# Dense products that read their moving operand in turn from its two halves

## The chip, the cores and the metric

The kernel runs on one core of one Trainium2 chip. The metric is the time of one execution in device microseconds (us); shorter is better. TensorE does the matrix products, VectorE, ScalarE and GpSimd the rest, and DMA queues bring the weights from the chip's main memory.

## The reference

A trunk of two layers works on 256 tokens of 1024 channels in float32. In each layer one input projection of the normalised stream feeds three token mixers: Mamba-2 (with a causal convolution of width 4 ahead of it), sliding-window attention with rotated queries and keys, and forgetting attention. Each has its own gate path, is projected back to 1024 channels, weighted by a sigmoid gate and summed; an output projection is added to the residual.

```python
for layer in range(DEPTH):
    h = rms_norm(x, norm_w[layer])
    proj = jnp.einsum('bsd,de->bse', h, w_in[layer])
    (a_xbc, a_z, a_dt, b_q, b_k, b_v, b_z,
     c_q, c_k, c_v, c_f, c_z, gates) = jnp.split(proj, split_at, axis=-1)
    y_a = mamba2_branch(a_xbc, a_z, a_dt, conv_w[layer], conv_b[layer], dt_bias[layer],
                        a_log[layer], d_skip[layer], ssm_norm_w[layer])
    y_b = sliding_window_branch(b_q, b_k, b_v, b_z, sinks[layer], cos, sin)
    y_c = forgetting_attention_branch(c_q, c_k, c_v, c_f, c_z, f_bias[layer])
    ys = jnp.stack([y_a, y_b, y_c], axis=2)
    branch = jnp.einsum('bsiw,iwd->bsid', ys, w_proj[layer])
    g = jax.nn.sigmoid(gates.reshape(b, s, N_BRANCH, d) + gate_bias[layer])
    merged = jnp.sum(g * branch, axis=2)
    x = x + jnp.einsum('bsd,de->bse', merged, w_out[layer])
return rms_norm(x, final_norm_w)
```

## The kernel before

Every dense product is computed to float32 accuracy from two-part operands. Weights and activations are split into a high part (type float32r) and the rest (also float32r): ScalarE copies the high part, VectorE subtracts it (`split`, lines 239 and 240). `dense` (line 254) then makes three matmuls for each of the eight blocks of 128 input channels: high by high, low by high, high by low. A product is thus 24 matmuls into one PSUM tile of the tag `mm`, of which there are three (`pmm`, line 71).

There are two orientations. `chan` (line 400) keeps 128 weight columns stationary and moves the activations, 256 tokens wide; its result has channels on the partitions and tokens along the row. The projections back (`u_proj`) do the same with the outputs of the mixers. `tok` (line 407) keeps 128 tokens stationary and moves the weights, 256 or 512 columns wide; its result has tokens on the partitions. It makes the sliding-window queries, keys and values, the values of forgetting attention, and the output projection. A small product (`u_small`) has 64 weight columns (two parts of 32) against 256 tokens. In all of them the moving operand is read word after word along a row.

Each product is followed by an eviction that reads its PSUM tile: a Tanh with a multiply-add for the gate paths (`u_z`: ScalarE line 727, then VectorE line 730 or, in the Mamba branch, 734), a Tanh for the sigmoid gates (`u_gate`, line 827), a multiply-add for the projections (`u_proj`, lines 847, 849, 855), ScalarE copies for keys, queries and values (lines 436, 773, 781, 791), the rotation (`rope`, lines 421 to 424, VectorE), and the residual sum (`u_out`, line 888, VectorE). The convolution (`u_conv`) reads the PSUM tile four times: a scaled copy with bias on ScalarE (line 640) and three multiply-adds on VectorE with the tokens shifted by 1, 2 and 3 (line 643).

TensorE's order is the program's. The dense products follow a written list (lines 938 to 1015); between them `pump` lets pieces of the attention and of the Mamba scan into TensorE's queue, by a clock that counts estimated TensorE time and by due times. The order on the other engines is the scheduler's, except at the start. Weights arrive on SP's DMA queue six pieces ahead; up to four split pieces are held. Small work tiles of 256 columns share the tag `L1`, with twelve buffers.

Of the kernel before, what the change touches and what calls it, by code (L numbers as in the profile page):

```python
# [16 lines left out]
P = 128  # L17
S = 256
# [25 lines left out]
def hybrid_trunk(  # L44
# [188 lines left out]
    def row_rstd(ss, n):  # L233
        return rsqrt(row_var(ss, n), 1)

    def split(hi, lo, src, scale=None):

        if scale is None:
            act(hi, src, AF.Copy)  # L239
            tt(lo, src, hi.bitcast(F32), op=ALU.subtract)  # L240
        else:
            act(hi, src, AF.Copy, scale=scale)  # L242
            stt(lo, src, scale, hi.bitcast(F32), op0=ALU.mult, op1=ALU.subtract)
# [156 lines left out]
    def chan(y, w, c):  # L400

        p = pmm()
        dense(p[:, 0:S], lambda k: w.hi(k)[:, c:c + P], lambda k: w.lo(k)[:, c:c + P],
              lambda k: y.hTh[:, k, :], lambda k: y.hTl[:, k, :], w)
        return p[:, 0:S]

    def tok(ah, al, w, t, p=None, **kw):

        n = w.n
        p = pmm() if p is None else p  # L410
        sl = slice(t * P, (t + 1) * P)
        dense(p[:, 0:n], lambda k: ah[:, k, sl], lambda k: al[:, k, sl], w.hi, w.lo, w,
              mid=pump if n == 512 else None, **kw)
        return p[:, 0:n]

    def rope(p, t):

# [9 lines left out]
    def u_bkv(y, c0, t, after=None):  # L427

        def f(w):
            p = tok(y.hTh, y.hTl, w, t, after=after)  # L430
            if t == 0 and c0 == 0:
                kv = T("L8", [P, 2048])
                y.kT = kv[:, 0:1024].rearrange("p (h s) -> p h s", h=4)
                y.bv = kv[:, 1024:1536].rearrange("p (t c) -> p t c", t=2)
            if c0 + w.n == 512:
                act(y.bv[:, t, :], p[:, w.n - 256:w.n], AF.Copy)
            if c0 == 0:
                a, b = rope(p[:, 0:256], t)
                kd = T("L2", [P, 4, 2, 64])
                for i in range(2):  # L440
                    gtt(kd[:, :, i, :], a, b, op=ALU.add)
                launch(1, rest(kd), D_K)
            pump()

        def rest(kd):
            pt = pmx()
            for h in range(4):
                transpose(pt[:, h * P:(h + 1) * P], kd[:, h, :, :].rearrange("p a b -> p (a b)"), ident)
            act(y.kT[:, :, t * P:(t + 1) * P], pt.rearrange("p (h s) -> p h s", h=4), AF.Copy)
            yield 0.0  # L450
        return f

    def u_bq(y, c0, t):

        def f(w):
            p = tok(y.hTh, y.hTl, w, t)
            for i in range(w.n // 256):
                if t == 0:
                    y.qT[c0 + i] = T("qt", [P, 2, S])
                a, b = rope(p[:, 256 * i:256 * i + 256], t)  # L460
                q = T("L1", [P, 4, 64])
                gtt(q, a, b, op=ALU.add)
                launch(1, rest(c0 + i, q.rearrange("p h d -> p (h d)")), D_Q)
            pump()

        def rest(c, q):
            qT = y.qT[c]
            pt = pmx()
            for j in range(2):
                transpose(pt[:, j * P:(j + 1) * P], q[:, j * P:(j + 1) * P], ident)  # L470
            act(qT[:, :, t * P:(t + 1) * P], pt[:, 0:256].rearrange("p (h s) -> p h s", h=2), AF.Copy)
            if t == 1:
                launch(1, swa_quad(y, c, qT), D_QK)
            yield 0.0
        return f
# [85 lines left out]
    def u_small(y):  # L561
        def f(w):

            p = pmm()
            for k in range(NK):
                for a in (y.hTh, y.hTl):
                    mm(p[0:64, 0:S], w.both[:, k, :], a[:, k, :], start=(k == 0 and a is y.hTh),
                       stop=(k == NK - 1 and a is y.hTl))
            raw = T("L1", [64, S])
            act(raw, p[0:64, 0:S], AF.Copy)  # L570
            launch(1, decay_logits(y, raw), 2.0)
            pump()
        return f
# [57 lines left out]
    def u_conv(y, u, c):  # L631
        def f(w):
            p = chan(y, w, c)
            if u == 8:
                y.bcT = T("L8", [P, 8, S])
            if u == 0:
                y.xs = T("L8", [P, 8, S])
            dst = y.xs[:, u, :] if u < 8 else y.bcT[:, u - 8, :]
            a = T("L1", [P, S])
            act(a, p, AF.Identity, scale=y.vec[:, 48 + u:49 + u], bias=y.vec[:, 64 + u:65 + u])  # L640
            for j in (2, 1, 0):
                s = 3 - j
                stt(a[:, s:S], p[:, 0:S - s], y.vec[:, 16 * j + u:16 * j + u + 1], a[:, s:S],  # L643
                    op0=ALU.mult, op1=ALU.add)
            th = T("L1", [P, S])
            act(th, a, AF.Tanh)  # L646
            stt(dst, th, 1.0, a, op0=ALU.add, op1=ALU.mult)
            if u < 8 and u % 2 == 1:
                launch(0, ssd_group(y, u // 2), D_G0)
            pump()  # L650
        return f
# [66 lines left out]
    def u_z(y, br, u, c):  # L718
        def f(w):
            p = chan(y, w, c)  # L720
            if u == 0 and br != 0:
                y.sz[br] = T("L8", [P, NK, S])
            if u == 0 and br == 0:
                y.yh[br] = T("L8", [P, NK, S], F32R)
                y.yl[br] = T("L8", [P, NK, S], F32R)
            th = T("L1", [P, S])
            act(th, p, AF.Tanh, scale=0.5)  # L727
            y.zdone.add(u) if br == 1 else None
            if br != 0:
                stt(y.sz[br][:, u, :], th, 1.0, p, op0=ALU.add, op1=ALU.mult)  # L730
            else:
                drain(0)
                sz = T("L1", [P, S])
                stt(sz, th, 1.0, p, op0=ALU.add, op1=ALU.mult)  # L734
                gtt(y.xs[:, u, :], y.xs[:, u, :], sz, op=ALU.mult)  # L735
                sq = T("L1", [P, S])
                act(sq, y.xs[:, u, :], AF.Square)  # L737
                y.sq.append(sq)
                if u % 2 == 1:
                    launch(3, group_norm(y, u // 2, *y.sq[-2:]), D_GN0)  # L740
            pump()
        return f
# [25 lines left out]
    def u_cv(y, c, t):  # L768
        def f(w):
            p = tok(y.hTh, y.hTl, w, t)  # L770
            if c == 0 and t == 0:
                y.cv = T("L8", [P, 2, D])
            act(y.cv[:, t, c:c + w.n], p, AF.Copy)
            pump()
        return f

    def u_ck(y, j, c):
        def f(w):
            p = chan(y, w, c)
            y.ckT[j] = T("qt", [P, 2, S])  # L780
            act(y.ckT[j][:, 0, :], p, AF.Copy)
            if j % 2 == 0:
                launch(2, fox_quad(y, j), D_FOX)
            pump()
        return f

    def u_cq(y, j, c):
        def f(w):
            p = chan(y, w, c)
            kq = y.ckT[j]  # L790
            act(kq[:, 1, :], p, AF.Copy)
            y.cqdone[j] = clock["t"]
            pump()
        return f
# [28 lines left out]
    def u_gate(y, br, u, c):  # L823
        def f(w):
            p = chan(y, w, c)
            g = T("L1", [P, S])
            act(g, p, AF.Tanh, scale=0.5, bias=y.vec[:, 88 + 8 * br + u:89 + 8 * br + u])  # L827
            y.gate[u] = g
            pump()
        return f  # L830

    def u_proj(y, br, u, c):
        def f(w):
            if u == 0:
# [3 lines left out]
                if br == 2:  # L838
# [2 lines left out]
            p = pmm()[:, 0:S]  # L841
            yh, yl = y.yh[br], y.yl[br]
            dense(p, lambda k: w.hi(k)[:, c:c + P], lambda k: w.lo(k)[:, c:c + P],
                  lambda k: yh[:, k, :], lambda k: yl[:, k, :], w)
            g = y.gate.pop(u)
            if br == 1:
                stt(y.mg[:, u, :], g, 1.0, p, op0=ALU.add, op1=ALU.mult)
            elif br == 0 or u < NK - 1:
                stt(g, g, 1.0, p, op0=ALU.add, op1=ALU.mult)  # L849
                gtt(y.mg[:, u, :], y.mg[:, u, :], g, op=ALU.add)  # L850
                if br == 2:
                    split(y.mh[:, u, :], y.ml[:, u, :], y.mg[:, u, :], scale=0.5)
            else:
                with tc.high_priority():
                    stt(g, g, 1.0, p, op0=ALU.add, op1=ALU.mult)
                    tt(y.mg[:, u, :], y.mg[:, u, :], g, op=ALU.add)
                    split(y.mh[:, u, :], y.ml[:, u, :], y.mg[:, u, :], scale=0.5)
            pump()
# [9 lines left out]
    def u_out(y, c, t, first=False, i=0):  # L868

        def f(w):  # L870
# [14 lines left out]
            else:  # L885
                p = tok(y.mh, y.ml, w, t)
            with tc.high_priority():
                tt(y.xn[:, t, sl], p, xo, op=ALU.add)
                sum_sq(y.xn, t, c, y.ss[t][:, i:i + 1], n)
                last = y.l + 1 == L  # L890
                nwb = fin["w"] if last else layers[y.l + 1].nwb
# [215 lines left out]
```

## Time and profile before

| | |
|---|---|
| median of 3 runs | 903.3 us (903.29 to 906.38) |
| profiled execution | 905.64 us, span 903.5 us |
| granted TensorE clock, mean | 0.99 |
| TensorE busy (matmul) | 884.3 us |
| VectorE busy | 628.8 us |
| ScalarE busy | 505.8 us |
| GpSimd busy | 136.0 us |
| read from main memory | 152.10 MB |

The profile gives, for one execution, the busy time of each engine, the chain of work that ended last (followed back from the last instruction), and groups of instructions by line, with their operands (`mm` is the PSUM tile of a dense product, `mx` that of the mixers' smaller products and transposes, `hi` and `lo` are weight parts, `L` stands for the work tiles L1 to L8), count, busy time, mean duration and the idle time ahead of them. PE is TensorE, PEld its weight loads, DVE VectorE, ACT ScalarE and POOL GpSimd. Matmuls overlap, so the mean duration of one is longer than its step to the next.

### The profile page before, as it was taken

How to read it: one execution, taken by the hardware profiler on the slowest of the kernel's cores; microseconds unless marked ns; L12 is line 12 of the kernel's file. 1: busy time of each engine (PE TensorE's matmuls, PEld its weight loads, DVE VectorE, ACT ScalarE, POOL GpSimd, SP SyncE). 2: the span in 40 equal slices, each digit the busy share in tenths (PEclk: the TensorE clock that was granted, in tenths of full speed). 3: DMA queues.
4: the chain of work that ended last, by engine and by line, in shares of the span. 5: the costliest groups of instructions: out<-in, count | busy, mean ns of one | idle time of the engine just before them, and what ended most of it. 6: DMA issues, size and time to landing. Idle time of an engine off the chain costs nothing.

```text
span 903.5 us, 18217 instructions
## 1 busy us (share of the span) xinstructions
PE 884.3 (98%) x7084; PEld 836.4 (93%) x7084; DVE 628.8 (70%) x1405; ACT 505.8 (56%) x990; POOL 136.0 (15%) x180
## 2 busy tenths in 40 slices
PE   6999999999999999999999999999999999999996
PEld 6899889999999989999888998899999999799995
DVE  5776888987665658646577788889667557775563
ACT  5465667655456647344454666675445665564442
POOL 5411000000010260222014010000000115213110
PEclk9999999999999999999999999999999999899999
DMA  8567445465556544548576465456655564346531
GB/s 285 172 211 232 134 151 174 162 207 160 157 173 184 152 154 140 162 148 266 182 236 208 137 193 163 139 157 195 190 185 158 172 184 146 113 141 186 186 118 70
DMA packets 149565, 155.43 MB, mean 172 GB/s; under 512 B 12616, under 2 KB 137256, under 8 KB 149480
## 3 DMA queue, kind: packets, MB, share of 16 engines
q1 hardware_dynamic: 134032, 140.79, 50.6%
q10 hardware_dynamic: 15400, 13.37, 4.7%
q8 instruction: 55, 0.90, 0.4%
q14 instruction: 30, 0.25, 0.1%
q0 software_dynamic: 48, 0.13, 0.0%
HBM read 152.10 MB, written 2.16 MB: 171 GB/s over the span
## 4 chain that ended last, share of the span: by engine, by line
PE 86%; issue 4%; DVE 4%; POOL 3%; ACT 1%; DMA 1%; POOLq 0%; SPq 0%; DVEq 0%; ACTq 0%
PE mm L96 76%; PE mx L96 7%; PE mx L100 3%; POOL L L735 2%; POOL sm L203 1%; DVE lo L240 1%; DMA L<-in_x_dram 1%; ACT hi L239 0%; DVE sm L205 0%; DVE L L734 0%; DVE L L764 0%; DVE L L240 0%; POOL L L745 0%; ACT L L737 0%; DVE pp L504 0%
## 5 line engine op out<-in xcount | busy, mean ns | idle before, releaser
L96 PE MATMUL mm<-L,hi 128*128 128x256 f32 x3328 | 610.9, 283 | 0.2 <-DVE L L240 0.2
L96 PEld LDWEIGHTS mm<-L,hi 128*128 128x128 f32 x3328 | 516.5, 189 | 7.9 <-issue 5.3
L96 PE MATMUL mm<-L,lo 128*128 128x256 f32 x1664 | 467.1, 281 | 0.0
L240 DVE TENSOR_TENSOR lo<-raw,hi 128x1024 fp32r<-128x1024 f32 x260 | 318.8, 1237 | 152.5 <-ACT hi L239 150.4
L239 ACT ACTIVATE hi<-raw 128x1024 fp32r<-128x1024 f32 x260 | 271.9, 1055 | 101.8 <-PE mm L96 68.5
L96 PEld LDWEIGHTS mm<-L,lo 128*128 128x128 f32 x1664 | 314.3, 189 | 0.1
L96 PE MATMUL mm<-hi,L 128*128 128x512 f32 (+1 forms) x576 | 149.6, 351 | 0.5 <-ACT L L239 0.2
L96 PEld LDWEIGHTS mm<-hi,L 128*128 128x128 f32 x576 | 98.8, 190 | 15.1 <-issue 0.7
L96 PE MATMUL mm<-lo,L 128*128 128x512 f32 (+1 forms) x288 | 98.9, 347 | 2.6 <-DVE lo L1039 2.6
L808 POOL TENSOR_SCALAR_AFFINE_SELECT bias<-bias 128x128 f32<-128x128 f32 x64 | 23.8, 410 | 460.4 <-DMA bias<-cumd 460.4
L510 ACT ACTIVATE pp<-pp,nm 128x128 f32<-128x128 f32 (+1 forms) x128 | 56.8, 445 | 21.2 <-DVE nm L504 21.1
L96 PEld LDWEIGHTS mm<-lo,L 128*128 128x128 f32 x288 | 54.2, 190 | 10.0 <-DVE lo L1039 2.8
L850 POOL TENSOR_TENSOR L<-L,L 128x256 f32<-128x256 f32 x30 | 33.6, 1119 | 130.0 <-DVE L L849 130.0
L643 DVE SCALAR_TENSOR_TENSOR L<-mm,vec,L 128x255 f32<-128x255 f32 (+2 forms) x96 | 45.9, 478 | 5.0 <-ACT L L640 3.4
L96 PE MATMUL mx<-L,L 128*64 128x128 f32 (+1 forms) x384 | 38.8, 329 | 4.4 <-DVE sm L751 3.5
L96 PEld LDWEIGHTS mx<-L,L 128*64 128x64 f32 x384 | 24.6, 142 | 15.5 <-DVE sm L751 3.7
L727 ACT ACTIVATE L<-mm 128x256 f32<-128x256 f32 x48 | 18.1, 378 | 31.7 <-PE mm L96 31.3
L522 DVE TENSOR_SCALAR pp<-pp,rsum 128x128 f32<-128x128 f32 (+1 forms) x128 | 32.4, 314 | 0.4
L827 ACT ACTIVATE L<-mm,vec 128x256 f32<-128x256 f32 x48 | 22.3, 468 | 17.3 <-PE mm L96 17.1
L646 ACT ACTIVATE L<-L 128x256 f32<-128x256 f32 x32 | 13.3, 415 | 32.8 <-DVE L L643 32.8
L539 ACT ACTIVATE L<-mx 128x512 f32<-128x512 f32 x48 | 27.1, 593 | 4.6 <-PE mx L100 2.9
L242 ACT ACTIVATE L<-L 128x256 fp32r<-128x256 f32 x16 | 6.7, 418 | 36.7 <-POOL L L850 32.4
(161 smaller groups left out, 711.8 us busy)
## 6 DMA issues: line engine op xcount, KB each, us to landing
raw<-in_w_in_dram SPq DMA_DIRECT2D x200, 512.0 KB, 4.2
raw<-in_w_proj_dram SPq DMA_DIRECT2D x48, 512.0 KB, 4.2
raw<-in_w_out_dram SPq DMA_DIRECT2D x16, 512.0 KB, 5.0
L<-cumd ACTq DMA_DIRECT2D x8, 512.0 KB, 5.4
bias<-cumd ACTq DMA_DIRECT2D x16, 256.0 KB, 3.7
L<-in_x_dram SPq DMA_DIRECT2D x2, 512.0 KB, 5.2
nwb<-in_norm_w_dram SPq DMA_DIRECT2D x1, 512.0 KB, 5.2
nwb<-in_norm_w_dram ACTq DMA_DIRECT2D x1, 512.0 KB, 6.6
```

The source lines that it names most:

```text
L96: nc.tensor.matmul(o, a, b, **kw)
L100: nc.tensor.transpose(o, a, i)
L239: act(hi, src, AF.Copy)
L240: tt(lo, src, hi.bitcast(F32), op=ALU.subtract)
L510: act(pp[:, i, sl], pp[:, i, sl], AF.Exp, scale=-1.0, bias=nm[:, e:e + 1], accum_out=sums[:, e:e + 1])
L522: ts(pp[:, i, sl], pp[:, i, sl], rs[:, 2 * i + b:2 * i + b + 1], 0.5, op0=ALU.mult, op1=ALU.mult)
L539: act(pT, pt, AF.Copy)
L643: stt(a[:, s:S], p[:, 0:S - s], y.vec[:, 16 * j + u:16 * j + u + 1], a[:, s:S], op0=ALU.mult, op1=ALU.add)
L727: act(th, p, AF.Tanh, scale=0.5)
L808: nc.gpsimd.affine_select(out=bias[:, i, dst], in_=bias[:, i, src], compare_op=ALU.is_ge, fill=NEG, base=0, pattern=[[-1, P]], channel_mul ...
L827: act(g, p, AF.Tanh, scale=0.5, bias=y.vec[:, 88 + 8 * br + u:89 + 8 * br + u])
L850: gtt(y.mg[:, u, :], y.mg[:, u, :], g, op=ALU.add)
```

## The change

The moving operand of the dense products is read through a view that takes columns 0, n/2, 1, n/2 + 1, and so on, in turn from the two halves of its n columns. The PSUM tile then holds the columns in that order. Each eviction reads it with a step of two words, first the even places (the first half), then the odd ones, and writes the halves one after the other, so that everything behind the evictions finds the old order. The sliding-window products whose rotation works on a tile of 256 columns (layer 0's keys, and the first and the last queries of layer 1) keep the old order. The convolution, which needs shifted tokens, gets an additional ScalarE copy `x_` of the PSUM tile into an `L1` tile in the old order, and its three multiply-adds read that copy instead of PSUM.

```diff
+    def in_turn(ap):
+        return ap.rearrange("p (a i) -> p i a", a=2)
+
+    def ordered(ap):
+        return ap.rearrange("p (i a) -> p a i", a=2)
+
+    def halves(ap):
+        return ap.rearrange("p (a i) -> p a i", a=2)
...
         dense(p[:, 0:S], lambda k: w.hi(k)[:, c:c + P], lambda k: w.lo(k)[:, c:c + P],
-              lambda k: y.hTh[:, k, :], lambda k: y.hTl[:, k, :], w)
-        return p[:, 0:S]
+              lambda k: in_turn(y.hTh[:, k, :]), lambda k: in_turn(y.hTl[:, k, :]), w)
+        return ordered(p[:, 0:S])
-    def tok(ah, al, w, t, p=None, **kw):
+    def tok(ah, al, w, t, p=None, turn=True, **kw):
...
-        dense(p[:, 0:n], lambda k: ah[:, k, sl], lambda k: al[:, k, sl], w.hi, w.lo, w,
-              mid=pump if n == 512 else None, **kw)
-        return p[:, 0:n]
+        b = in_turn if turn else lambda ap: ap
+        dense(p[:, 0:n], lambda k: ah[:, k, sl], lambda k: al[:, k, sl], lambda k: b(w.hi(k)),
+              lambda k: b(w.lo(k)), w, mid=pump if n == 512 else None, **kw)
+        return ordered(p[:, 0:n]) if turn else p[:, 0:n]
...
-            p = tok(y.hTh, y.hTl, w, t, after=after)
+            p = tok(y.hTh, y.hTl, w, t, turn=w.n == 512 or c0 > 0, after=after)
...
-            p = tok(y.hTh, y.hTl, w, t)
+            p = tok(y.hTh, y.hTl, w, t, turn=w.n == 512)
...
-                a, b = rope(p[:, 256 * i:256 * i + 256], t)
+                a, b = rope(p if w.n == 256 else p[:, i, :], t)
...
-                    mm(p[0:64, 0:S], w.both[:, k, :], a[:, k, :], start=(k == 0 and a is y.hTh),
+                    mm(p[0:64, 0:S], w.both[:, k, :], in_turn(a[:, k, :]), start=(k == 0 and a is y.hTh),
...
-            act(a, p, AF.Identity, scale=y.vec[:, 48 + u:49 + u], bias=y.vec[:, 64 + u:65 + u])
+            x_ = T("L1", [P, S])
+            act(halves(x_), p, AF.Copy)
+            act(halves(a), p, AF.Identity, scale=y.vec[:, 48 + u:49 + u], bias=y.vec[:, 64 + u:65 + u])
             for j in (2, 1, 0):
                 s = 3 - j
-                stt(a[:, s:S], p[:, 0:S - s], y.vec[:, 16 * j + u:16 * j + u + 1], a[:, s:S],
+                stt(a[:, s:S], x_[:, 0:S - s], y.vec[:, 16 * j + u:16 * j + u + 1], a[:, s:S],
...
-            act(th, p, AF.Tanh, scale=0.5)
+            act(halves(th), p, AF.Tanh, scale=0.5)
...
-                stt(y.sz[br][:, u, :], th, 1.0, p, op0=ALU.add, op1=ALU.mult)
+                stt(halves(y.sz[br][:, u, :]), halves(th), 1.0, p, op0=ALU.add, op1=ALU.mult)
...
-                  lambda k: yh[:, k, :], lambda k: yl[:, k, :], w)
+                  lambda k: in_turn(yh[:, k, :]), lambda k: in_turn(yl[:, k, :]), w)
+            p = ordered(p)
...
-                tt(y.xn[:, t, sl], p, xo, op=ALU.add)
+                tt(halves(y.xn[:, t, sl]), p, halves(xo), op=ALU.add)
```

The evictions left out here (the other multiply-adds of the gates and projections, the copies of keys, queries and values) change in the same way.

More of the change, by code (lines that the diff above doesn't have):

```diff
@@ L434, in f @@
                 y.bv = kv[:, 1024:1536].rearrange("p (t c) -> p t c", t=2)
-            if c0 + w.n == 512:
-                act(y.bv[:, t, :], p[:, w.n - 256:w.n], AF.Copy)
+            if c0 > 0:
+                act(halves(y.bv[:, t, :]), p, AF.Copy)
+            elif w.n == 512:
+                act(y.bv[:, t, :], p[:, 1, :], AF.Copy)
             if c0 == 0:
-                a, b = rope(p[:, 0:256], t)
+                a, b = rope(p if w.n == 256 else p[:, 0, :], t)
                 kd = T("L2", [P, 4, 2, 64])
@@ L566, in f @@
                 for a in (y.hTh, y.hTl):
-                    mm(p[0:64, 0:S], w.both[:, k, :], a[:, k, :], start=(k == 0 and a is y.hTh),
+                    mm(p[0:64, 0:S], w.both[:, k, :], in_turn(a[:, k, :]), start=(k == 0 and a is y.hTh),
                        stop=(k == NK - 1 and a is y.hTl))
             raw = T("L1", [64, S])
-            act(raw, p[0:64, 0:S], AF.Copy)
+            act(halves(raw), ordered(p[0:64, 0:S]), AF.Copy)
             launch(1, decay_logits(y, raw), 2.0)
@@ L733, in f @@
                 sz = T("L1", [P, S])
-                stt(sz, th, 1.0, p, op0=ALU.add, op1=ALU.mult)
+                stt(halves(sz), halves(th), 1.0, p, op0=ALU.add, op1=ALU.mult)
                 gtt(y.xs[:, u, :], y.xs[:, u, :], sz, op=ALU.mult)
@@ L772, in f @@
                 y.cv = T("L8", [P, 2, D])
-            act(y.cv[:, t, c:c + w.n], p, AF.Copy)
+            act(halves(y.cv[:, t, c:c + w.n]), p, AF.Copy)
             pump()
@@ L780, in f @@
             y.ckT[j] = T("qt", [P, 2, S])
-            act(y.ckT[j][:, 0, :], p, AF.Copy)
+            act(halves(y.ckT[j][:, 0, :]), p, AF.Copy)
             if j % 2 == 0:
@@ L790, in f @@
             kq = y.ckT[j]
-            act(kq[:, 1, :], p, AF.Copy)
+            act(halves(kq[:, 1, :]), p, AF.Copy)
             y.cqdone[j] = clock["t"]
@@ L826, in f @@
             g = T("L1", [P, S])
-            act(g, p, AF.Tanh, scale=0.5, bias=y.vec[:, 88 + 8 * br + u:89 + 8 * br + u])
+            act(halves(g), p, AF.Tanh, scale=0.5, bias=y.vec[:, 88 + 8 * br + u:89 + 8 * br + u])
             y.gate[u] = g
@@ L843, in f @@
             dense(p, lambda k: w.hi(k)[:, c:c + P], lambda k: w.lo(k)[:, c:c + P],
-                  lambda k: yh[:, k, :], lambda k: yl[:, k, :], w)
+                  lambda k: in_turn(yh[:, k, :]), lambda k: in_turn(yl[:, k, :]), w)
+            p = ordered(p)
             g = y.gate.pop(u)
+            g2 = halves(g)
             if br == 1:
-                stt(y.mg[:, u, :], g, 1.0, p, op0=ALU.add, op1=ALU.mult)
+                stt(halves(y.mg[:, u, :]), g2, 1.0, p, op0=ALU.add, op1=ALU.mult)
             elif br == 0 or u < NK - 1:
-                stt(g, g, 1.0, p, op0=ALU.add, op1=ALU.mult)
+                stt(g2, g2, 1.0, p, op0=ALU.add, op1=ALU.mult)
                 gtt(y.mg[:, u, :], y.mg[:, u, :], g, op=ALU.add)
@@ L854, in f @@
                 with tc.high_priority():
-                    stt(g, g, 1.0, p, op0=ALU.add, op1=ALU.mult)
+                    stt(g2, g2, 1.0, p, op0=ALU.add, op1=ALU.mult)
                     tt(y.mg[:, u, :], y.mg[:, u, :], g, op=ALU.add)
```

## The prediction

> **What bounds the kernel now.** I read the page first: the busy time of the engines, the granted clock, the chain that ended last.
>
> ```profile
> span 903.5 us, 18217 instructions
> PE 884.3 (98%) x7084; PEld 836.4 (93%) x7084; DVE 628.8 (70%) x1405; ACT 505.8 (56%) x990; POOL 136.0 (15%) x180
> ...
> PEclk9999999999999999999999999999999999899999
> ...
> PE 86%; issue 4%; DVE 4%; POOL 3%; ACT 1%; DMA 1%; POOLq 0%; SPq 0%; DVEq 0%; ACTq 0%
> PE mm L96 76%; PE mx L96 7%; PE mx L100 3%; POOL L L735 2%; POOL sm L203 1%; DVE lo L240 1%; DMA L<-in_x_dram 1%; ACT hi L239 0%; DVE sm L205 0%; DVE L L734 0%; DVE L L764 0%; DVE L L240 0%; POOL L L745 0%; ACT L L737 0%; DVE pp L504 0%
> ```
>
> TensorE is busy for 98% of the span at full granted clock, and three quarters of the chain are its dense products into `mm` (line 96). VectorE and ScalarE have 30% and 44% of the span to spare. So the change is priced by what it does to one dense matmul, times their number. The number comes from the groups of instructions, with shapes kept apart:
>
> ```profile
> L96 PE MATMUL mm<-L,hi 128*128 128x256 f32 x3328 | 610.9, 283 | 0.2 <-DVE L L240 0.2
> L96 PE MATMUL mm<-L,lo 128*128 128x256 f32 x1664 | 467.1, 281 | 0.0
> L96 PE MATMUL mm<-hi,L 128*128 128x512 f32 x320 | 102.1, 399 | 0.5 <-ACT L L239 0.2 <-DVE L L240 0.2
> L96 PE MATMUL mm<-lo,L 128*128 128x512 f32 x160 | 63.3, 396 | 0.0
> L96 PE MATMUL mm<-hi,L 128*128 128x256 f32 x256 | 47.8, 290 | 0.0
> L96 PE MATMUL mm<-lo,L 128*128 128x256 f32 x128 | 35.6, 286 | 2.6 <-DVE lo L1039 2.6
> L96 PE MATMUL mm<-L,L 128*64 128x256 f32 x32 | 4.2, 283 | 0.0
> ```
>
> That is 3328 + 1664 = 4992 matmuls whose moving operand is activations of 256 columns, 480 whose moving operand is 512 weight columns, 384 with 256 weight columns, and 32 of the small product. The last column is idle time before them: TensorE waits some 3 us for all of them together, so evictions do not hold it up.
>
> The means of 280 to 400 ns are latencies of overlapping matmuls. What one matmul costs is the step from one to the next, and that I take from the chain in order of time (start, length, what), in stretches where nothing else runs on TensorE; the rows behind it say which shape the stretch at 31 us and the one at 160 us have.
>
> ```profile
> 31.23 0.44 PE mx L100 x4
> 31.67 8.40 PE mm L96 x36
> 40.07 0.44 PE mx L100 x4
> ...
> 160.78 11.40 PE mm L96 x96
> 186.66 11.27 PE mm L96 x96
> ```
>
> ```profile
> L96 PE MATMUL mm<-hi,L 128*128 128x512 f32 x26 | 8.4, 403 | 0.0
> L96 PE MATMUL mm<-lo,L 128*128 128x512 f32 x14 | 5.5, 392 | 0.0
> ...
> L96 PE MATMUL mm<-L,hi 128*128 128x256 f32 x64 | 11.6, 282 | 0.0
> L96 PE MATMUL mm<-L,lo 128*128 128x256 f32 x32 | 9.0, 281 | 0.0
> ```
>
> With 512 columns a step is 8.40 / 36 = 233.3 ns; with 256 columns 11.40 / 96 = 118.8 and 11.27 / 96 = 117.4, mean 118.1. Twice the columns cost 1.98 times as much although each matmul loads its weights once in both shapes. So the columns of the moving operand set the pace, at 0.46 ns each, not the weight loads. The transposes (plain float32 data) take 0.44 / 4 = 110 ns for 128 columns, 0.86 ns each: that is the one row here in which TensorE takes a column much more slowly than in a dense product. Half of it, 0.43 ns or 110 ns for 256 columns and 220 for 512, is a little below what the dense products reach; they lose 8 and 13 ns a matmul against it.
>
> **The change part by part.** *The moving operand.* `in_turn` makes neighbours in the stream lie 128 words (512 bytes) apart, or 256 words (1024 bytes) for 512 columns; no two neighbours in the stream lie side by side in memory. It applies to all 480 wide matmuls, all 4992 with activations, the 32 of the small product, and of the 384 with 256 weight columns to those outside the rotary products. Those left alone are layer 0's key product and layer 1's first and last query product, each with 24 matmuls for either half of the tokens: 3 x 48 = 144, which leaves 240. So 5264 matmuls of 256 columns and 480 of 512 are read in turn; counts of matmuls, weights and bytes do not change.
>
> No dense matmul of this trace reads a moving operand with a gap between neighbours, so the price is bounded by the rows above. The low end is the half transpose: 110 and 220 ns, a gain of 8.1 x 5264 + 13.3 x 480 = 49 us. The middle is the transpose's own 0.86 ns a column: 220 and 440 ns, a loss of 101.9 x 5264 + 206.7 x 480 = 536 + 99 = 636 us. If one read now brings two adjacent words, reading in turn brings one useful word per read, and the doubling is of today's steps: 118.1 x 5264 + 233.3 x 480 = 734 us. I take 636 us. The reason: a 4-byte column every 0.46 ns is slower than the 0.43 ns of the same array on transposes, which need a new column only half as often. So the dense stream already seems to be held by the reading of its operand, and an order that uses less of each read has nothing to fall back on. It is an inference; the trace has no strided row to confirm it.
>
> [...]
>
> *The evictions* read PSUM with every second word and write in order. These are the ones concerned (the three rows of the rotation stand for its wide products only):
>
> ```profile
> L727 ACT ACTIVATE L<-mm 128x256 f32<-128x256 f32 x48 | 18.1, 378 | 31.7 <-PE mm L96 31.3 <-issue 0.4
> L827 ACT ACTIVATE L<-mm,vec 128x256 f32<-128x256 f32 x48 | 22.3, 468 | 17.3 <-PE mm L96 17.1
> L640 ACT ACTIVATE L<-mm,vec 128x256 f32<-128x256 f32 x32 | 17.8, 555 | 6.9 <-PE mm L96 6.5
> L791 ACT ACTIVATE qt<-mm 128x256 f32<-128x256 f32 x16 | 6.2, 386 | 12.2 <-PE mm L96 12.2
> L781 ACT ACTIVATE qt<-mm 128x256 f32<-128x256 f32 x16 | 6.0, 378 | 14.4 <-PE mm L96 14.4
> L773 ACT ACTIVATE L<-mm 128x512 f32<-128x512 f32 x8 | 4.7, 583 | 1.3 <-PE mm L96 1.3
> L730 DVE SCALAR_TENSOR_TENSOR L<-L,mm 128x256 f32<-128x256 f32 x32 | 13.3, 414 | 9.7 <-ACT L L727 9.7
> L849 DVE SCALAR_TENSOR_TENSOR L<-L,mm 128x256 f32<-128x256 f32 x30 | 12.5, 417 | 6.2 <-PE mm L96 6.2
> L734 DVE SCALAR_TENSOR_TENSOR L<-L,mm 128x256 f32<-128x256 f32 x16 | 6.7, 417 | 7.2 <-ACT L L727 7.0
> L847 DVE SCALAR_TENSOR_TENSOR L<-L,mm 128x256 f32<-128x256 f32 x16 | 6.6, 413 | 2.9 <-PE mm L96 2.9
> L421 DVE TENSOR_TENSOR L<-mm,rope 128x256 f32<-128x256 f32 x20 | 8.4, 418 | 7.8 <-PE mm L96 6.9 <-ACT L L436 0.8
> L423 DVE TENSOR_TENSOR L<-mm,rope 128x128 f32<-128x128 f32 x20 | 5.6, 279 | 0.0
> ```
>
> From 378 ns at 256 elements and 583 at 512, a ScalarE element costs 0.80 ns; from 279 at 128 and 418 at 256, a VectorE element 1.09. A step of two words costs between nothing and a second element time: 0.20 us for a ScalarE eviction of 256, 0.28 us for one on VectorE. At the dear end that is 160 x 0.20 + 8 x 0.41 = 35 us on ScalarE and 94 x 0.28 = 26 us on VectorE, with the rotation and the residual sums some 38. *The convolution* adds one ScalarE copy per channel tile, 32 x 0.378 (as L727) = 12 us, or 19 at the dear step, and its three shifted multiplies read SBUF instead of PSUM. Altogether ScalarE goes from 506 to at most 560 us and VectorE from 629 to at most 667, of 903. The cover is three `mm` buffers: a product of 24 matmuls lasts 24 x 118 = 2.8 us, so an eviction may be 2 us later before TensorE notices. The copy stands ahead of the scaled one on ScalarE; the first shifted multiply on VectorE and the next weight split on ScalarE queue behind it. As the PSUM tile is let go after two ScalarE reads instead of after the third multiply, its buffer comes free earlier, not later. The convolution holds three of the twelve `L1` tiles instead of two; beside tiles that gates hold it may wait for one, between 0 and 2.8 us at two places per layer; I take 0.
>
> Where nothing covers an eviction is the drained stretch before the last gate products, and the end:
>
> ```profile
> POOL L L735 <- DVE L L734: 36.8, 8, 7.8
> 887.97 0.44 DVE L L888
> ```
>
> There the 16 instructions of line 734 stand on or near the chain: 16 x 0.28 = 4.5 us, and 0.3 us for line 888, so 5 us. With TensorE twice as slow this drowns in its work, so the forecast takes none of it.
>
> *Sum.* The profiled execution took 905.64 us, of which 903.5 are span; 905.64 + 636 = 1541. It lies 2.3 us above the median of the runs, 903.3, so against that 903.3 + 636 = 1539 us.
>
> **The rivals.** *Full speed: faster.* The dense steps lose 8 and 13 ns against the half transpose, more with more columns, so something in the reading of adjacent words costs. If it is that a fetch of adjacent words has to finish before the next starts, two places read in turn could overlap, and the loss goes: 903.3 - 49 + 5 = 859 us. It decides once the step falls below 117 ns (5 us over 5744 matmuls is 0.9 ns each). For it speaks that the loss is there, grows with columns and stays with clock granted; against it, that each place then gives one word per visit. [...]
>
> *Rate unchanged.* The array takes any order as fast, and the uncovered evictions remain: 903.3 + 5 = 908 us. For it speaks that one column is one address either way; against it, the dense rate below the transposes' pace.
>
> *A smaller loss*, as a lost column time for every second column: half of 636, 1221 us. *A larger one*, if a word takes four column times: 440 and 880 ns, 322 x 5264 + 647 x 480 = 2005 us more, 2908 us.
>
> **How the numbers follow.** Chances: two column times each 0.40, the smaller loss 0.08, the larger 0.05, rate unchanged 0.12, full speed 0.35. Within 0.5% (4.5 us, about what a measurement of this kernel can tell from no change) takes 0.05 of the unchanged rate, the rest of it is slower by more: slower 0.40 + 0.08 + 0.05 + 0.07 = 0.60, same 0.05, faster 0.35. The likeliest case alone spans 1500 (the 19 us in which TensorE idles, and as much of the other engines' share of the chain, going under) to 1640 (doubling of today's step). Both signs hold much of the chance, so the range goes from 850, just under the full-speed case, to 1640; only the larger loss and the edges lie outside.
>
> **What would show it.** Right: stretches of 96 matmuls of 256 columns in the chain take about 21 us instead of 11.4, 36 of 512 columns about 15.8 instead of 8.40; TensorE stays above 95% busy and ScalarE and VectorE fall to about 36% and 43% of the longer span; the evictions of lines 727 and 730 take up to 0.58 and 0.69 us with no wait of TensorE behind them. The forecast is wrong if the 256-column step stays at or below 120 ns; below 112 the full-speed rival is right, and then the evictions decide how much of 49 us arrives. If the step is unchanged and the time grows by over 10 us, I mis-sized the cover of evictions or of the `L1` tiles.

## The result, and the profile after

The changed kernel takes 868.52 us (median of 4 runs, 866.89 to 870.85) against 903.67 for the kernel before (with a fourth run beside the three above): a ratio of 0.9607, 95% interval 0.9576 to 0.9637. It is 35 us faster where 636 us slower was forecast. The page after has the same engine on top and the same granted clock, 0.99.

```profile
span 865.6 us, 18241 instructions
...
PE 844.7 (98%) x7084; PEld 803.2 (93%) x7084; DVE 623.6 (72%) x1405; ACT 508.6 (59%) x1022; POOL 137.4 (16%) x180
...
PEclk9999999999999989999999999999999999899999
...
PE 81%; DMA 5%; DVE 4%; issue 3%; ACT 3%; POOL 3%; ACTq 0%; SPq 0%; POOLq 0%; DVEq 0%
PE mm L96 69%; PE mx L96 9%; DMA raw<-in_w_in_dram 4%; PE mx L100 3%; ACT hi L252 2%; DVE lo L253 2%; POOL L L871 1%; DMA raw<-in_w_proj_dram 1%; POOL L L754 1%; DMA L<-in_x_dram 1%; POOL sm L203 0%; DVE L L870 0%; DVE L L909 0%; ACT L L215 0%; ACT L L255 0%
```

TensorE has 39.6 us less busy time with the same 7084 matmuls, the span is 37.9 us shorter, and the arrival of weights (DMA) now holds 5% of the chain instead of 1%. The medians lie 35 us apart and the profiled executions 38: the one before, 905.64 us, was 2 us above its median, the one after, 867.64, 0.9 below. The steps stand in the chain in order of time (start, length, what):

```profile
28.10 0.44 PE mx L100 x4
28.54 6.49 PE mm L96 x30
38.56 12.05 DMA raw<-in_w_in_dram
153.73 10.72 PE mm L96 x96
178.25 10.72 PE mm L96 x96
```

A transpose still takes 110 ns. A dense matmul of 512 columns takes 6.49 / 30 = 216 ns instead of 233, one of 256 columns 10.72 / 96 = 111.7 instead of 118.1. Over the counts of the prediction that is 17 x 480 + 6.4 x 5264 = 42 us. Set side by side, matmul by matmul, the two traces give 41.4 us from ordinary steps; 19 places whose step changed by over 150 ns take back 3.6 us on balance. Most of those that grew are waits that the faster TensorE now reaches. Two are shown below from the list of waits after (us in total, times, longest): the group normalisation, whose wait was 3.5 us before, and four transposes of the queries, which did not wait before. The transposes wait for a sum on GpSimd; in the chain the weights above stand ahead of it, through their split and the rotation on VectorE.

```profile
PE mx L96 <- DVE sm L770: 5.2, 2, 2.6
PE mx L100 <- POOL L L479: 1.7, 4, 0.6
```

The evictions, in the groups with shapes kept apart (line 746 was 727, 749 was 730, 753 was 734, 792 was 773, 870 was 849, 659 was 640; 658 is the new copy):

```profile
L746 ACT ACTIVATE L<-mm 128x256 f32<-128x256 f32 x48 | 18.1, 377 | 25.8 <-PE mm L96 25.3 <-issue 0.4
L749 DVE SCALAR_TENSOR_TENSOR L<-L,mm 128x256 f32<-128x256 f32 x32 | 13.3, 416 | 5.3 <-ACT L L746 5.3
L870 DVE SCALAR_TENSOR_TENSOR L<-L,mm 128x256 f32<-128x256 f32 x30 | 12.5, 417 | 3.9 <-PE mm L96 3.9
L658 ACT ACTIVATE L<-mm 128x256 f32<-128x256 f32 x32 | 11.9, 372 | 1.4 <-PE mm L96 1.4
L659 ACT ACTIVATE L<-mm,vec 128x256 f32<-128x256 f32 x32 | 18.0, 562 | 0.0
L753 DVE SCALAR_TENSOR_TENSOR L<-L,mm 128x256 f32<-128x256 f32 x16 | 6.7, 418 | 9.3 <-ACT L L746 9.3
L792 ACT ACTIVATE L<-mm 128x512 f32<-128x512 f32 x8 | 4.7, 585 | 0.0
```

377 ns against 378, 416 against 414, 417 against 417, 585 against 583: reading every second word of PSUM costs these evictions nothing. The largest difference among the evictions is that of the convolution's scaled copy, 562 ns against 555, 0.2 us over its 32.

### The profile page after: what moved, and what is told of

Same layout as the page of the kernel before. It is cut to its first block, busy times and chain, and to the rows that moved or that the text cites. A ratio compares the mean times of both kernels' runs of the same rounds, so it can differ in the third digit from the quotient of the medians.

```text
span 865.6 us, 18241 instructions
## 1 busy us (share of the span) xinstructions
PE 844.7 (98%) x7084; PEld 803.2 (93%) x7084; DVE 623.6 (72%) x1405; ACT 508.6 (59%) x1022; POOL 137.4 (16%) x180
## 4 chain that ended last, share of the span: by engine, by line
PE 81%; DMA 5%; DVE 4%; issue 3%; ACT 3%; POOL 3%; ACTq 0%; SPq 0%; POOLq 0%; DVEq 0%
PE mm L96 69%; PE mx L96 9%; DMA raw<-in_w_in_dram 4%; PE mx L100 3%; ACT hi L252 2%; DVE lo L253 2%; POOL L L871 1%; DMA raw<-in_w_proj_dram 1%; POOL L L754 1%; DMA L<-in_x_dram 1%; POOL sm L203 0%; DVE L L870 0%; DVE L L909 0%; ACT L L215 0%; ACT L L255 0%
## 5 line engine op out<-in xcount | busy, mean ns | idle before, releaser
L96 PE MATMUL mm<-L,hi 128*128 128x256 f32 x3328 | 579.3, 278 | 0.0
L96 PE MATMUL mm<-L,lo 128*128 128x256 f32 x1664 | 458.5, 276 | 0.0
L96 PEld LDWEIGHTS mm<-L,lo 128*128 128x128 f32 x1664 | 320.3, 192 | 0.1
L96 PE MATMUL mm<-hi,L 128*128 128x512 f32 (+1 forms) x576 | 142.5, 339 | 2.2 <-ACT L L255 1.1
L96 PE MATMUL mm<-lo,L 128*128 128x512 f32 (+1 forms) x288 | 95.6, 335 | 1.4 <-DVE lo L1060 1.0
L827 POOL TENSOR_SCALAR_AFFINE_SELECT bias<-bias 128x128 f32<-128x128 f32 x64 | 25.8, 439 | 436.1 <-DMA bias<-cumd 436.1
L662 DVE SCALAR_TENSOR_TENSOR L<-L,vec,L 128x255 f32<-128x255 f32 (+2 forms) x96 | 46.2, 481 | 3.0 <-ACT L L659 1.8
```

The source lines that it names most:

```text
L96: nc.tensor.matmul(o, a, b, **kw)
L662: stt(a[:, s:S], x_[:, 0:S - s], y.vec[:, 16 * j + u:16 * j + u + 1], a[:, s:S], op0=ALU.mult, op1=ALU.add)
L827: nc.gpsimd.affine_select(out=bias[:, i, dst], in_=bias[:, i, src], compare_op=ALU.is_ge, fill=NEG, base=0, pattern=[[-1, P]], channel_mul ...
```

## The experiments

**The change taken apart.** Two kernels each do one part of it. `act_only` turns the activations but not the weights:

```diff
-        b = in_turn if turn else lambda ap: ap
+        b = lambda ap: ap
...
-        return ordered(p[:, 0:n]) if turn else p[:, 0:n]
+        return halves(p[:, 0:n]) if turn else p[:, 0:n]
```

> The changed kernel with the order in turn for activations alone (4992 matmuls and the small product); the weights move in plain order. Theory 1 (all of the gain is a lower step of each turned matmul): the 480 wide ones go back from 216 to 233 ns and 240 of 256 columns from 112 to 119, 10 us more than the changed kernel, 878 to 879 us. Rival (the gain comes from a few stages or from the freed PSUM buffers of the convolution): unchanged, 868.

Measured: 874.87 us, ratio 0.9685 (0.967 to 0.9699). Its chain has both steps side by side, 8.40 / 36 = 233 ns for the wide ones left plain and 111.7 for the others:

```profile
29.18 8.40 PE mm L96 x36
154.80 10.72 PE mm L96 x96
```

So each turned matmul carries its own gain. The activations bring 28 us; the weights bring 6 to 7 of the 10 forecast for them. Side by side, the traces of `act_only` and of the changed kernel differ by 7.8 us of ordinary steps, of which larger waits take back 1.3.

`rest_only` keeps the evictions and the copy and reads the moving operand word after word, so its columns are out of order behind the evictions:

```diff
     def in_turn(ap):
-        return ap.rearrange("p (a i) -> p i a", a=2)
+        return ap
```

> The changed kernel with the moving operand read in plain order; its evictions still read every second word and the convolution still gets its copy (so columns are out of order behind the evictions). It prices the change's other half. Theory 1: evictions with a step cost nothing on their engines (377 ns against 378 measured), the copy adds 12 us to ScalarE off the path: 901 to 906 us, no change against the kernel before. Rival (the copy lets PSUM go early and gives part of the gain): under 898. Rival (the copy and the evictions stand on the path and the rate alone would have brought more): 908 or more.

Measured: 902.07 us, ratio 0.9992 (0.9982 to 1.0002). The steps are those of the kernel before, and the evictions stay at 377 and 414 ns:

```profile
158.85 11.40 PE mm L96 x96
184.73 11.27 PE mm L96 x96
```

All that the change adds around the products costs nothing that can be measured at the old step, and it brings nothing either. The gain comes from the reading order.

**Which property of the order.** `orders` gives eight orders to different groups of products, each by a matmul on its own line (the comments, which the kernel does not have, give the line):

```diff
+        halves=order("p (a i) -> p i a", a=2),        # line 116
+        quarters=order("p (a i) -> p i a", a=4),      # line 120
+        eighths=order("p (a i) -> p i a", a=8),       # line 124
+        pairs=order("p (a i b) -> p i a b", a=2, b=2),    # line 128
+        runs4=order("p (a i b) -> p i a b", a=2, b=4),    # line 132
+        runs16=order("p (a i b) -> p i a b", a=2, b=16),  # line 136
+        step2=order("p (i a) -> p a i", a=2),         # line 140
+        step16=order("p (i a) -> p a i", a=16))       # line 144
```

> The kernel before, with eight different reading orders of the moving operand given to different groups of dense products, each by a matmul of its own line; evictions take the columns as they come, so tokens end up in another order in those products, and only steps are read from it. Groups of 256 columns: step2 (even words, then odd ones, one stream), step16 (every 16th word, one stream), halves, quarters and eighths in turn (single words from 2, 4, 8 places), pairs, runs of 4 and runs of 16 words in turn from two halves; plain for one gate group and the projections. Of 512 columns: step2 (queries) and pairs (values). Theory N (neighbours: what costs is that adjacent words follow each other): step2, step16, halves, quarters and eighths take 111.7 ns a matmul, pairs, runs of 4 and runs of 16 keep 117 to 119. [...] At 512 columns fast is 216, slow 233.

Measured, in the chain of that kernel (line 96 is plain):

```profile
105.96 10.88 PE mm L140 x48
...
214.74 8.13 PE mm L128 x48
...
255.95 11.40 PE mm L96 x96
...
287.46 5.81 PE mm L136 x48
...
313.68 10.56 PE mm L144 x48
325.12 6.87 PE mm L120 x48
...
398.65 10.66 PE mm L124 x48
...
454.73 5.36 PE mm L116 x48
...
494.83 12.16 PE mm L132 x96
```

Per matmul: halves 111.7 ns, plain 118.8, runs of 16 121, runs of 4 126.7, quarters 143, pairs 169, step16 220, eighths 222, step2 227. Theory N does not survive: it wanted step2, step16, quarters and eighths at 111.7 ns, and they take 143 to 227. As a whole this kernel took 1117 us in its single run, which says nothing by itself: it is read for its steps alone.

`psum_pairs` applies pairs to every dense matmul, and writes PSUM in the same two places:

```diff
+    def in_turn(ap):
+        return ap.rearrange("p (a i b) -> p i a b", a=2, b=2)
...
-            mm(pt, a(k), b(k), start=(ks[0] == 0 and i == 0), stop=(ks[1] == NK and i == len(seq) - 1))
+            mm(in_turn(pt), a(k), in_turn(b(k)), start=(ks[0] == 0 and i == 0), stop=(ks[1] == NK and i == len(seq) - 1))
```

> The kernel before with one edit: every dense matmul reads its moving operand in pairs of words in turn from the two halves and writes PSUM in the same places, so the columns lie in order there and evictions and convolution stay as before, and all products are turned, 5888. [...] Theory N: adjacent words still follow each other, so 117 to 119 ns, 903 us. Theory W (writes to PSUM in two places cost): above 910 us.

Measured: 1206.9 us, ratio 1.3364 (1.3341 to 1.3386).

```profile
198.24 8.15 PE mm L96 x48
208.53 15.79 PE mm L96 x96
243.44 15.79 PE mm L96 x96
```

The step is 164.5 ns in the long stretches. It looks like theory W, but the group of pairs in `orders`, which writes PSUM in order, has 169 ns. That group is the convolution's, and its own products take 8.15 / 48 = 170 ns here (the row at 198 us): the reading costs, and the writing in two places adds nothing that shows. Theory N's 117 to 119 ns is not near it.

**Words in a row.** The ranking fits a count. Take the even columns of the stream and the odd ones as two sequences, divide a row of the operand into groups of four neighbouring words, and count how many words each sequence takes in a row from one group. Plain order has two and takes 118.8 ns; so have runs of 16 and runs of 4, with 121 and 126.7. Halves has four, with 111.7. Step2, step16 and eighths have one, with 227, 220 and 222; in pairs and quarters (169 and 143) each sequence takes single words by turns from two groups. By this count, single words in turn from two neighbouring blocks of 4, 8 or 32 words (weave4, weave8, weave32) belong with halves. With plain order belong weave2 and hits2 (every second word of the two halves in turn, in two passes), with step2 hits1 (every fourth word, in four passes). The count describes measured steps; what in the hardware stands behind it, no run shows. `orders2` tests it against the distance between the two places (D), and reads the weights at every second column in one group:

```diff
+        halves=order("p (a i) -> p i a", a=2),             # line 115
+        weave2=order("p (i a j) -> p i j a", a=2, j=2),    # line 119
+        weave4=order("p (i a j) -> p i j a", a=2, j=4),    # line 123
+        weave8=order("p (i a j) -> p i j a", a=2, j=8),    # line 127
+        weave32=order("p (i a j) -> p i j a", a=2, j=32),  # line 131
+        hits2=order("p (a i l) -> p l i a", a=2, l=2),     # line 135
+        hits1=order("p (a i l) -> p l i a", a=2, l=4))     # line 139
...
+            p = chan(y, w, c, mm_halves, lambda h, c: h.rearrange("p (i a) -> p a i", a=2)[:, c // P, :])
```

> The kernel before with a second set of reading orders, each with a line of its own; evictions take the columns as they come, so tokens (and for the queries of forgetting attention channels) are out of order and only steps are read. [...] Theory D (distance: two places read in turn must be 512 bytes or more apart; eighths at 128 bytes took 222, quarters at 256 bytes 143): hits1 and hits2 keep the distance of the halves, 111.7; weave4, weave8 and weave32 are too near, 220 or so. Halves for one gate group is the control, 111.7; plain for another, 118. Halves with weights read at every second column: 111.7 if the weight loads don't mind, above 150 if they do as the moving words do.

Measured in its chain (one run, 940 us as a whole); the row of line 123 is of 512 columns, and line 115 at 252 us is the group with weights at every second column:

```profile
126.93 5.18 PE mm L123 x24
137.86 5.70 PE mm L135 x48
144.21 5.70 PE mm L96 x48
...
215.67 5.36 PE mm L131 x48
...
240.19 11.09 PE mm L139 x48
252.16 5.75 PE mm L115 x48
...
365.34 5.64 PE mm L119 x48
...
421.88 5.36 PE mm L115 x48
...
779.39 5.36 PE mm L127 x48
```

| order | words in a row from one group of four, even and odd columns each | ns at 256 columns |
|---|---|---|
| halves; weave8, weave32 | four | 111.7 |
| plain; weave2; hits2 | two | 118.8; 117.5; 118.8 |
| runs16; runs4 (from `orders`) | two | 121; 126.7 |
| hits1 | one | 231 |
| step16; eighths; step2 (from `orders`) | one | 220; 222; 227 |

Weave4 at 512 columns takes 5.18 / 24 = 216 ns, as halves do. Every order lands where the count put it; hits1 lies 2 to 5% above the others that have one. Hits1 and hits2 are read in turn from the same two places as the halves, and take 231 and 118.8 ns; weave8 and weave32 lie 32 and 128 bytes apart and keep 111.7. So neither distance nor the number of places orders these steps, and the count does. The weights at every second column make a turned matmul of 256 columns 119.8 ns instead of 111.7, neither the 111.7 nor the more than 150 of the expectation. So the order in which the weights are read moves the step as well: by 8 ns, against 119 for moving words in order hits1, but enough to lose the gain.

**A check on the whole kernel.** `all_turned` is the changed kernel with weights read in turn from neighbouring blocks of 32 words, 128 bytes apart, and with the 144 matmuls turned that the change left plain:

```diff
+    def turn32(ap):
+        return ap.rearrange("p (g a i) -> p g i a", a=2, i=32)
...
-        b = in_turn if turn else lambda ap: ap
+        b = turn32
```

> The changed kernel, with the products that move weights reading them in turn from neighbouring blocks of 32 words (128 bytes apart) instead of from the two halves; 32 is half a head, so the rotation can read its PSUM tile in that order and the 144 matmuls left plain by the change are turned too: all 5888. [...] Theory D (distance): the 480 wide and 384 narrow weight matmuls near 450 and 225 ns, some 130 us slower than the changed kernel.

> The changed kernel on the same chip as the version with all products turned, for a comparison within one batch: 868 us, a ratio of 0.961 to the kernel before; 111.7 and 216 ns a step.

Measured: 867.45 us, ratio 0.9603 (0.9584 to 0.9623); the changed kernel beside it 868.14 us, ratio 0.961 (0.959 to 0.963). By the measured steps the 144 newly turned matmuls are worth 144 x 8.3 ns = 1.2 us. That and the 0.7 measured between the two are too small for these intervals, so it isn't shown to be better than the changed kernel. But theory D would have had it far slower: by its steps of 450 and 225 ns some 155 us (the 130 of the expectation is too low). The row at 94 us is of the wide products that move weights, 5.18 / 24 = 216 ns; the rows at 154 and 178 us move activations. The row at 468 us is the last query product of layer 1, 48 of the 144: 5.36 / 48 = 111.7 ns, against 5.76 / 48 = 120 in the changed kernel (its row at 467.54 us).

```profile
94.82 5.18 PE mm L96 x24
154.08 10.72 PE mm L96 x96
178.60 10.72 PE mm L96 x96
...
468.04 5.36 PE mm L96 x48
```

## Why the prediction was wrong

**What bounds the kernel** was right: the time moved with the step of the dense matmuls, and the counts of 5264 and 480 with the measured steps give 42 us, which with 3.6 us more of waits is the 38 us of span. The chain's stretches of 36 and 96 matmuls were the right ones to watch.

**The price of the moving operand** is the step that failed. It took a transpose's 0.86 ns a column, 220 and 440 ns; measured were 111.7 and 216, near the low end of the bounds that stood beside it (110 and 220). That low end, half of a transpose, was an estimate, and the wide step lies below it; that one read brings two words, the ground for 734 us, no run shows. The narrow step lies just below the 112 ns that the prediction gave as the sign for its rival of full speed. The failing argument was that the dense stream is held by reading its operand, so that an order which uses less of each read can only lose. The transposes were not the only slow row either: in the trace before, the mixers' sixteen matmuls of 256 plain float32 columns (`mx<-L,bt`), read word after word and in pairs, start 217 ns apart within a pair, the same 0.85 ns a column. So the price was that of rows with another type of data, not of a reading order. The argument's first half agrees with the runs: two orders that differ only in the places they read differ in step, 111.7 and 118.8 ns. The second half does not follow: neighbours 512 bytes apart are not a worse order than neighbours side by side. The step2 and hits1 groups show that the size of the feared loss came out near by luck, 227 and 231 ns against the 220 forecast, for orders whose even and odd columns take one word of a group of four at a time. In turn from two halves is not such an order; by the measured steps it is a better one than plain.

**The rival of full speed** was right as far as the loss against the half transpose went: 1.7 ns of 8 are left at 256 columns, none of 13 at 512. Its overlap of two places does not explain that: hits1 and hits2, in turn from the same two places, take 231 and 118.8 ns. Its 859 us came out at 868.5: the narrow step is 111.7 instead of 110 (9 us), the wide one 216 instead of 220 (2 us the other way), the 5 us of evictions are not there, and 3.6 us of waits are. That makes 865; most of the rest is that the two profiled executions lie 38 us apart and the medians 35. Its "below 117 ns" was the right place to decide. The narrow step is more than half of the wide one, 111.7 against 108. The small product, with 64 weight columns, steps by 109 after the change (from the starts of its matmuls), those with 128 weight columns by 111.7. The author's guess is that the loading of weights holds the narrow dense matmuls now, as weights at every second column bring 119.8; only that was tried.

**Evictions and the copy** were priced between nothing and 35 + 38 us on the engines and 12 to 19 for the copy; measured were nothing for the step of two words and 12 us for the copy, off the path. Taking 5 us for the uncovered ones was too much: the interval of `rest_only` reaches from 1.6 us faster to 0.2 us slower. No wait for an `L1` tile came up: the copy's idle time, 1.4 us, ends with TensorE alone.

**The chances.** Full speed had 0.35 against 0.40. The reason given for 0.40 was an inference from one row about another kind of data, and the row that spoke for the rival, a loss that grows with columns at full granted clock, was as near. The low end, 850, did reach the result's side; it took no part in the forecast.

What stays open: why quarters and pairs, whose even and odd columns take single words by turns from two groups of four, need 143 and 169 ns a matmul, both less than the 220 to 231 of the orders that count one. The count ranks fifteen orders: it was made from nine of them, and the other six came out as it put them. Why the step follows it, no run shows.

## What to carry to other kernels

The step of the dense matmuls grew with its columns and lay above half of what plain float32 data take in the same kernel (118 and 233 ns against 110 and 220), and another order of the moving operand took 6 to 17 ns off it. Where a profile shows the same, the order is worth a trial: one kernel with a different order for each group of products answers for a dozen orders at once. For these float32r operands the best orders gave even and odd columns each their own run of at least four neighbouring words (111.7 ns at 256 columns); plain order cost 6 to 8% more (118.1 against 111.7, 233.3 against 216), and one word at a time doubled the step (220 to 231). A result that comes out permuted was put in order by evictions with a step of two words at no measured cost (377 ns against 378), and `rest_only` found none for the whole of it (ratio 0.9992).

## What the runs showed of the hardware

- A dense matmul whose float32r moving operand was read word after word took 118.1 and 233.3 ns for 256 and 512 columns, against 111.7 and 216 in turn from two runs of four or more words.
- Single words at a step took 220 to 231 ns at 256 columns, for steps of 8 bytes (step2), 16 bytes (in turn, hits1) and 64 bytes (step16) alike.
- Evictions on ScalarE and VectorE read every second word of PSUM as fast as every word (377 against 378 ns, 416 against 414).
- Writing a product to PSUM in pairs of words at two places cost nothing that shows (170 ns against 169 for the same products, read alike and written in order).
